# A hybrid encoder layer on one core: the last blocks of three products in seven instead of eight block products, and their streamed hi parts made by ScalarE

## The chip, the cores and the metric

The kernel runs on one core of one Trainium2 chip. The metric is the device time of one execution in microseconds (us); smaller is better. Five engines work side by side, each through a queue of its own in the order in which the program was built: TensorE (PE, with its weight loads as PEld), VectorE (DVE), ScalarE (ACT), GpSimd (POOL) and SyncE (SP, which issues nearly all DMAs). They wait for one another through semaphores only.

## What is computed

One layer on 2048 tokens of width 1024, all in fp32, cut to what matters:

```python
u = rms_norm(h, g_mix_pre);  z = u @ w_in
y = concat(swa_with_sinks(...z...), hgrn2(...z...)) @ w_out          # out projection
h = h + rms_norm(y, g_mix_post)
u = rms_norm(h, g_x_pre);  m = rms_norm(mem, g_mem)
y = softmax((u @ wq) (m @ wk).T per head) (m @ wv) @ wo              # cross-attention, 4 heads, 256 memory tokens
h = h + rms_norm(y, g_x_post)
u = rms_norm(h, g_ffn_pre)
y = (silu(u @ w_gate) * (u @ w_up)) @ w_down
h = h + rms_norm(y, g_ffn_post)
```

## The kernel before

**Precision.** TensorE multiplies in the fast fp32r format. Each fp32 matrix is split into a hi part (rounded to fp32r) and a lo part (the rest); a product is hi x hi + hi x lo + lo x hi, three matmuls. In `products` these are lines 1122, 1123 and 1124. A split is `split2`: the hi part at line 985 (`engine="A"`, ScalarE) or line 987 (POOL), then the lo part by a VectorE subtraction at line 988.

**The folded cross-attention.** Before the stage of interest, `fold_cross` multiplies wq with the memory's keys and wo with its values, so that scores and values are two products with 1024 x 1024 matrices (`qk_d`, `vo_d`). Out projection, scores, values, gate/up and down are then all of one form: a resident matrix of 1024 x 1024 (or less) against a stream.

**Seven products.** A block takes 256 columns of the stream and multiplies them with the resident matrix, both cut into 2 x 2 parts. In plain form ("p", `eight`) that is eight products of parts; each has four k tiles (`nk`), so 12 matmuls of 128x512. In Strassen-Winograd form ("s", `seven`) it is seven, with sums of parts on both sides:

```python
STEPS = {"s": (1, 5, 6, 3, 7, 2, 4), "p": (1, 2, 8, 3), ...}
```

The numbers name the residents: 1, 2, 3 and 8 are parts, 5, 6, 7 and 4 are sums of parts. A step of "s" is one product, a step of "p" two. `streamed` makes the block's stream tiles `S`: for "p" four splits, for "s" four sums (line 1097) and seven splits. Five `S` buffers take turns; tiles are made two steps ahead (`upto(need[g + 2])`). `seven` copies three partial results out of PSUM (`part`, line 1137), and each job's `out` adds them on VectorE.

**Jobs.** `jobs` lists the stage: out projection (`mixed_block`), scores (`score_block`), values (`value_block`), gate/up for two halves of the tokens (`hidden_blocks`), down in three parts (`down_block`). The first three have 8 blocks of 256 tokens each. Their streams come from `tokens`. The blocks' kinds come from `kinds`: out projection's first block is "p", the last block of each of the first three jobs is "p", every other block of the stage is "s". The down and gate/up jobs already name "s" for their last blocks, and give "A" to `streamed`, so that ScalarE makes all hi parts; in the first three jobs `streamed` gives four of the seven hi parts of a block to ScalarE and three to POOL.

**Residents.** `phases` keeps seven slots for residents: four "big" and three "T" tiles. `half` loads one half of the next resident (128x1024) when a slot's last use is past; `split` splits it (ScalarE hi, VectorE lo, a 128x1024 operation each) two steps later, queued behind what the step issued before. Where a job's last block is "s" (`change`), more halves and splits are allowed for in that block and the next job's first (`fresh`). The sums 5, 7, 6 and 4 are made ahead by `combined` and loaded ready.

**Beside the products** each block has row work, spread over the following steps (`after`): root mean squares (ScalarE squares at line 1476, small POOL operations at lines 1487 to 1491), scalings and residual adds on VectorE (lines 1529, 1530, 1604, 1608, 1617), for scores the maxima (1561), exps (ScalarE, 1565) and divisions (1573), and transposes (TensorE 1381, ScalarE copy 1382). The scheduler of the framework fixes each engine's order from these when the program is built.

Of the kernel before, what the change touches and what calls it, by code (L numbers as in the profile page):

```python
# [29 lines left out]
NT = T // P  # L30
# [18 lines left out]
class Layer:  # L49
# [1121 lines left out]
    def plain(self, S, T, nk, out, keep, kind):  # L1171
# [36 lines left out]
        yield  # L1208

    def phases(self, jobs, first, prologue=None):  # L1210

        steps = [(n, i, p) for n, job in enumerate(jobs) for i, b in enumerate(job[2])
                 for p in self.STEPS[b[0]]]
        takes = [c for job in jobs for b in job[2] for c in self.TAKES[b[0]]]
# [200 lines left out]
    def jobs(self):  # L1418
        I = self.I

        def weights(src, r0, nk):
            return lambda t, i, j, k0, n: self.load(
                t, src[r0 + (i * nk + k0) * P:r0 + (i * nk + k0 + n) * P, j * 512:(j + 1) * 512]
                .rearrange("(k p) d -> p k d", p=P))

        def ffn_u(b):
            return lambda t, i, j, k0, n: self.load(
                t, self.u_d[4 * i + k0:4 * i + k0 + n, :, b * TB + j * 512:b * TB + (j + 1) * 512]
                .rearrange("k p t -> p k t"))

        def kinds(blocks, n=0, last="p"):
            return [("p" if i < n else last if i == len(blocks) - 1 else "s",) + b for i, b in enumerate(blocks)]

        def sums(name, src, nk, other=None):
            return self.sums(name, src, nk, self.extra_tile, other or self.gain_tile)

        def in_turn(*what):
            return lambda: itertools.chain.from_iterable(w() for w in what)

        qk, vo = weights(self.qk_d, 0, 4), weights(self.vo_d, 0, 4)  # L1440
        down = [(weights(I["w_down"], f0 * P, nk), f0, nk) for f0, nk in ((0, 3), (6, 4), (14, 4))]
        qk_s, vo_s = sums("qk_s", qk, 4, self.row_tile), sums("vo_s", vo, 4)
        u_s = sums("u_s", ffn_u(1), 4)
        self.u0_s = self.tc.dram_tile([4, P, 4 * 512], F32, name="u0_s")
        d_s = [sums(f"d_s{c}", src, nk) for c, (src, _, nk) in enumerate(down)]
        jobs = [(self.w_out, 4, kinds([self.mixed_block(n) for n in range(0, NT, 2)], 1), self.out_sums, {1: [qk_s[1]]}),
                (qk, 4, kinds([self.score_block(n) for n in range(0, NT, 2)]), qk_s[0], {1: [vo_s[1]]}),
                (vo, 4, kinds([self.value_block(n) for n in range(0, NT, 2)]), vo_s[0], {})]
        for b in range(NB):
            beside = {2: [in_turn(*(d[1] for d in d_s))]} if b else {4: [u_s[1]]}  # L1450
            jobs.append((ffn_u(b), 4, kinds([blk for f in range(0, NFF, 2) for blk in self.hidden_blocks(b, f)], 0, "s"),
                         u_s[0] if b else self.u0_s, beside))
        for c, (src, f0, nk) in enumerate(down):
            jobs.append((src, nk, kinds([self.down_block(c, f0, nk, n) for n in range(0, NT, 2)], 0, "s"), d_s[c][0], {}))

        return jobs
# [10 lines left out]
    def tokens(self, src, n):  # L1467

        return lambda kind: self.streamed(lambda t, j: self.load(
            t, src[n:n + 2, :, 512 * j:512 * j + 512].rearrange("i p c -> p i c")), 4, kind, tiles=True)  # L1470

    def mean_square(self, a, to):

# [291 lines left out]
```

## Time and profile before

| | |
|---|---|
| time, median of 3 runs | 2574.08 us (2572.68 to 2574.33) |
| profiled execution: time, span | 2572.97 us, 2571.3 us |
| TensorE clock granted | 0.999 |
| PE, DVE, ACT, POOL busy | 2535.4, 1764.8, 1263.9, 425.4 us |
| first matmul of out projection, scores, values, gate/up | 778.8, 952.2, 1122.9, 1295.2 us |
| first matmul of the second gate/up job | 1720.7 us |

The profile comes from one execution. A group's line names the source line, engine, operation, tile written and read, and the count; behind the bar stand busy us, mean ns of one, and the idle time of that engine just before, with what ended it. Lengths of operations that follow each other overlap a little, and a matmul's modelled length overlaps the next ones, so paces are read from start to start. Idle time of an engine that is not the bottleneck costs nothing.

### The profile page before, as it was taken

Reading aid. Unit: us, or ns where it says so; the run is one execution under the profiler, and the core shown is the slowest. Engines: PE = TensorE matmul, PEld = TensorE weight load, DVE = VectorE, ACT = ScalarE, POOL = GpSimd, SP = SyncE. Lnnn points to the kernel's source line nnn. Section 1 sums busy time; section 2 is a strip of 40 time slices with the busy share of each in tenths; the row PEclk is TensorE's granted clock in tenths of the full one; section 3 lists DMA queues with packets and bytes.
Section 4 is the critical chain, followed back from the end, with each engine's and each line's share of the span. In section 5 each row is a group of like instructions: output and inputs, shape, how many; then the busy total and the mean of one; then the engine's idle time right before and its main releaser. Section 6 shows DMA issues by size and latency. Waiting matters only on the chain.

```text
span 2571.3 us, 34876 instructions
## 1 busy us (share of the span) xinstructions
PE 2535.4 (99%) x12326; PEld 2124.0 (83%) x12326; DVE 1764.8 (69%) x2791; ACT 1263.9 (49%) x2643; POOL 425.4 (17%) x612
## 2 busy tenths in 40 slices
PE   9999999999999999999999999999999999999998
PEld 8888888878987888888778888888888888888886
DVE  7785588887556778788885655576666557574766
ACT  5563466555555565565563333344333335443543
POOL 4231334321312322212310000000000000000022
PEclk9999999999999999999999999999999999999999
DMA  5445755765887896665973622253555425464776
GB/s 189 148 164 170 205 162 163 228 198 160 262 282 276 294 310 209 221 218 198 341 244 117 205 91 74 82 205 117 186 197 196 156 94 182 165 195 106 226 178 152
DMA packets 357295, 486.36 MB, mean 189 GB/s; under 512 B 20352, under 2 KB 248704, under 8 KB 357120
## 3 DMA queue, kind: packets, MB, share of 16 engines
q1 hardware_dynamic: 351072, 462.11, 54.6%
q0 software_dynamic: 6048, 22.02, 4.9%
q8 instruction: 97, 1.59, 0.3%
q14 instruction: 78, 0.64, 0.1%
HBM read 317.34 MB, written 166.72 MB: 188 GB/s over the span
## 4 chain that ended last, share of the span: by engine, by line
PE 82%; DMA 6%; DVE 6%; ACT 2%; issue 2%; POOL 1%; SPq 1%; DVEq 0%; POOLq 0%; ACTq 0%
PE psm L1122 22%; PE psm L1124 22%; PE psm L1123 22%; PE psg L157 2%; PE psg L156 2%; PE psg L158 2%; PE pss L1381 1%; DMA x<-in_w_out_dram 1%; DVE S L988 1%; DMA y_d<-sg 1%; DMA u_d<-row 1%; DVE T L988 0%; SPq L75 0%; DMA qk_s<-extra 0%; DVE S L808 0%
## 5 line engine op out<-in xcount | busy, mean ns | idle before, releaser
L1123 PE MATMUL psm<-T,S 128*128 128x512 f32 x2680 | 1042.9, 390 | 1.4 <-DVE T L988 1.4
L1122 PE MATMUL psm<-T,S 128*128 128x512 f32 x2680 | 1035.2, 391 | 4.9 <-ACT part L1137 3.4
L1124 PE MATMUL psm<-T,S 128*128 128x512 f32 x2680 | 1030.5, 390 | 4.9 <-DVE S L988 4.9
L1122 PEld LDWEIGHTS psm<-T,S 128*128 128x128 f32 x2680 | 503.0, 188 | 113.3 <-ACT part L1137 6.0
L1124 PEld LDWEIGHTS psm<-T,S 128*128 128x128 f32 x2680 | 503.1, 188 | 111.4 <-DVE S L988 7.0
L1123 PEld LDWEIGHTS psm<-T,S 128*128 128x128 f32 x2680 | 503.2, 188 | 106.4 <-DVE T L988 3.8
L985 ACT ACTIVATE S<-sum 128x512 fp32r<-128x512 f32 (+1 forms) x330 | 198.6, 619 | 364.1 <-PE psm L1124 260.9
L988 DVE TENSOR_TENSOR S<-sraw,S 128x512 fp32r<-128x512 f32 (+1 forms) x315 | 214.6, 689 | 229.8 <-ACT S L985 216.4
L988 DVE TENSOR_TENSOR S<-sum,S 128x512 fp32r<-128x512 f32 (+1 forms) x388 | 259.1, 677 | 47.1 <-ACT S L985 32.6
L1137 ACT ACTIVATE part<-psm 128x512 f32<-128x512 f32 x285 | 168.9, 596 | 244.9 <-PE psm L1124 223.6
L985 ACT ACTIVATE S<-sraw 128x512 fp32r<-128x512 f32 (+1 forms) x268 | 165.2, 617 | 110.0 <-PE psm L1124 99.4
L1509 POOL DMA_DIRECT2D y_d<-row x16 | 14.0, 877 | 1077.4 <-DVE row L1695 1026.6
L988 DVE TENSOR_TENSOR T<-row,T 128x1024 fp32r<-128x1024 f32 (+1 forms) x112 | 131.8, 1189 | 35.9 <-ACT T L985 34.1
L157 PE MATMUL psg<-u,whi 128*128 128x512 f32 x320 | 127.8, 399 | 0.0
L158 PE MATMUL psg<-u,wlo 128*128 128x512 f32 x320 | 127.1, 397 | 0.0
L156 PE MATMUL psg<-u,whi 128*128 128x512 f32 x320 | 127.1, 397 | 0.0
L1476 ACT ACTIVATE junk<-row 128x512 f32<-128x512 f32 x160 | 99.7, 625 | 45.7 <-DVE row L1498 27.2
L985 ACT ACTIVATE T<-row 128x1024 fp32r<-128x1024 f32 (+1 forms) x112 | 113.6, 1032 | 8.6 <-DMA row<-d_s 4.3
L987 POOL TENSOR_SCALAR S<-sum 128x512 fp32r<-128x512 f32 x58 | 49.4, 851 | 300.1 <-PE psm L1124 240.9
L1646 DVE TENSOR_TENSOR row<-psm,part 128x512 f32<-128x512 f32 x66 | 43.7, 688 | 68.3 <-PE psm L1124 68.2
L1655 DVE TENSOR_TENSOR part<-psm,part 128x512 f32<-128x512 f32 x66 | 43.8, 688 | 60.2 <-PE psm L1124 60.0
L1695 DVE TENSOR_TENSOR row<-psm,part 128x512 f32<-128x512 f32 x72 | 49.1, 688 | 49.5 <-PE psm L1124 49.4
(364 smaller groups left out, 3715.6 us busy)
## 6 DMA issues: line engine op xcount, KB each, us to landing
sraw<-in_w_gate_dram SPq DMA_DIRECT2D x44, 512.0 KB, 3.6
sraw<-in_w_up_dram SPq DMA_DIRECT2D x44, 512.0 KB, 3.7
hid_d<-row SPq DMA_DIRECT2D x44, 512.0 KB, 2.7
sraw<-hid_d SPq DMA_DIRECT2D x32, 512.0 KB, 4.1
sraw<-in_w_in_dram SPq DMA_DIRECT2D x44, 256.0 KB, 3.6
z_d<-pair SPq DMA_DIRECT2D x20, 512.0 KB, 3.0
raw<-in_w_in_dram SPq DMA_DIRECT2D x20, 512.0 KB, 4.6
z_d<-z SPq DMA_DIRECT2D x20, 512.0 KB, 4.0
```

The source lines that it names most:

```text
L156: nc.tensor.matmul(ps, ah, bh, start=(i == 0), stop=False)
L157: nc.tensor.matmul(ps, ah, bl, start=False, stop=False)
L158: nc.tensor.matmul(ps, al, bh, start=False, stop=(i == n - 1))
L985: self.nc.scalar.activation(hi, raw, AF.Copy)
L987: self.nc.gpsimd.tensor_scalar(hi, raw, 1.0, 1.0, ALU.mult, ALU.mult)
L988: self.nc.vector.tensor_tensor(lo, raw, f32(hi), ALU.subtract)
L1122: nc.tensor.matmul(ps, s[:, 0, k, :], t[:, 0, k, :], start=st, stop=False, **kw)
L1123: nc.tensor.matmul(ps, s[:, 0, k, :], t[:, 1, k, :], start=False, stop=False, **kw)
L1124: nc.tensor.matmul(ps, s[:, 1, k, :], t[:, 0, k, :], start=False, stop=sp, **kw)
L1137: nc.scalar.activation(t, ps, AF.Copy)
L1476: self.nc.scalar.activation(junk, a, AF.Square, scale=float(D) ** -0.5, accum_out=to)
L1695: nc.vector.tensor_tensor(d, a, b, ALU.add)
```

## The change

In `jobs` the last blocks of out projection, scores and values become "s"; in `tokens` the stream of these three jobs is given to `streamed` with "A".

```diff
-        jobs = [(self.w_out, 4, kinds([self.mixed_block(n) for n in range(0, NT, 2)], 1), self.out_sums, {1: [qk_s[1]]}),
-                (qk, 4, kinds([self.score_block(n) for n in range(0, NT, 2)]), qk_s[0], {1: [vo_s[1]]}),
-                (vo, 4, kinds([self.value_block(n) for n in range(0, NT, 2)]), vo_s[0], {})]
+        jobs = [(self.w_out, 4, kinds([self.mixed_block(n) for n in range(0, NT, 2)], 1, "s"), self.out_sums, {1: [qk_s[1]]}),
+                (qk, 4, kinds([self.score_block(n) for n in range(0, NT, 2)], 0, "s"), qk_s[0], {1: [vo_s[1]]}),
+                (vo, 4, kinds([self.value_block(n) for n in range(0, NT, 2)], 0, "s"), vo_s[0], {})]
...
         return lambda kind: self.streamed(lambda t, j: self.load(
-            t, src[n:n + 2, :, 512 * j:512 * j + 512].rearrange("i p c -> p i c")), 4, kind, tiles=True)
+            t, src[n:n + 2, :, 512 * j:512 * j + 512].rearrange("i p c -> p i c")), 4, kind, "A", tiles=True)
```

What follows from it in the code: with "s" last, `steps` grows by three a job, resident 8 is fetched a second time in none of the three jobs, and `change` and `fresh` hold at these three changes of job too. The parts of the program that the scheduler orders around them move as well.

## The prediction

> **What bounds the kernel now.** I read the page's engine line first.
>
> ```profile
> PE 2535.4 (99%) x12326; PEld 2124.0 (83%) x12326; DVE 1764.8 (69%) x2791; ACT 1263.9 (49%) x2643; POOL 425.4 (17%) x612
> ```
>
> TensorE works 99% of the span, so the time is the number of its matmuls plus a few waits. Two rows of TensorE's timeline, twelve matmuls (one block product of four k tiles, three matmuls each) apart, give the pace:
>
> ```profile
> 797.84 0.39 PE L1122 MATMUL psm<-T,S 128*128 128x512 f32 x1
> ...
> 800.56 0.39 PE L1122 MATMUL psm<-T,S 128*128 128x512 f32 x1
> ```
>
> That is 2.72 us a product, 0.227 us a matmul; the 0.39 is the pipelined length of one. Next the busy times by stage, cut at the first matmul of each job (columns: length; busy PE, weight loads, DVE, ACT, POOL; clock; DMA share, GB/s), and what PE waited for in the first three jobs:
>
> ```profile
> 778.80:952.20 173.40, 170.62 (x801) 141.00 (x800) 125.04 (x147) 97.36 (x215) 45.88 (x68) 1.00 0.84 291
> 952.20:1122.90 170.70, 170.70 (x823) 142.41 (x822) 137.24 (x234) 100.74 (x236) 47.12 (x66) 1.00 0.71 238
> 1122.90:1295.20 172.30, 169.33 (x798) 139.69 (x797) 145.79 (x183) 104.66 (x232) 48.12 (x66) 1.00 0.74 245
> 1295.20:1720.70 425.50, 423.98 (x1882) 349.75 (x1881) 259.83 (x379) 174.16 (x303) 4.37 (x6) 1.00 0.43 142
> ...
> PE psm L1124 <- DVE S L988: 4.9, 4, 2.3
> PE psm L1123 <- DVE T L988: 1.4, 3, 0.8
> PE psm L1122 <- ACT part L1137: 0.7, 1, 0.7
> ```
>
> The rows are out projection, scores, values, first gate/up job. In the first three VectorE is 72 to 85% busy and PE waits 7.0 us in all; in the fourth VectorE is 61% busy. So TensorE sets the time, but VectorE stands close behind it exactly in the three jobs that the change touches. What it does there, by form, from 830 to 1300 us (count, then busy us and mean ns):
>
> ```profile
> L1476 ACT ACTIVATE junk<-row 128x512 f32<-128x512 f32 x112 | 69.6, 623 | 26.7 <-DVE row L1498 24.8 <-DVE row L1608 0.9 <-DVE row L1557 0.2
> L988 DVE TENSOR_TENSOR S<-sum,S 128x512 fp32r<-128x512 f32 x75 | 51.0, 684 | 9.0 <-POOL S L987 7.6 <-ACT S L985 0.7
> L988 DVE TENSOR_TENSOR S<-sraw,S 128x512 fp32r<-128x512 f32 x68 | 48.9, 722 | 20.1 <-ACT S L985 12.4 <-POOL S L987 7.6
> L988 DVE TENSOR_TENSOR T<-row,T 128x1024 fp32r<-128x1024 f32 x40 | 48.4, 1219 | 11.4 <-ACT T L985 11.3
> L1382 ACT ACTIVATE row<-pss 128x512 f32<-128x512 f32 x84 | 46.2, 591 | 7.8 <-PE pss L1381 7.8
> L985 ACT ACTIVATE T<-row 128x1024 fp32r<-128x1024 f32 x43 | 44.5, 1057 | 0.0
> L1137 ACT ACTIVATE part<-psm 128x512 f32<-128x512 f32 x56 | 32.3, 593 | 29.0 <-PE psm L1124 28.6 <-DVE row L1557 0.3
> L987 POOL TENSOR_SCALAR S<-sum 128x512 fp32r<-128x512 f32 x36 | 30.8, 855 | 166.0 <-PE psm L1124 135.4 <-DVE S L988 15.7 <-DVE sum L1097 8.1
> L987 POOL TENSOR_SCALAR S<-sraw 128x512 fp32r<-128x512 f32 x27 | 26.5, 983 | 46.6 <-PE psm L1124 37.7 <-issue 6.8 <-ACT part L1137 2.1
> L985 ACT ACTIVATE S<-sum 128x512 fp32r<-128x512 f32 x40 | 24.9, 630 | 37.0 <-PE psm L1124 31.4 <-issue 5.5
> L1565 ACT ACTIVATE row<-row,x_mr,r_x 128x256 f32<-128x256 f32 x42 | 24.9, 594 | 32.9 <-POOL x_mr L1563 32.7
> L1573 DVE TENSOR_SCALAR row<-row,mc 128x256 f32<-128x256 f32 x64 | 19.3, 364 | 0.2
> L1530 DVE TENSOR_TENSOR row<-row,row 128x1024 f32<-128x1024 f32 x14 | 18.7, 1362 | 0.0
> L1529 DVE SCALAR_TENSOR_TENSOR row<-row,q_r,g 128x1024 f32<-128x1024 f32 x14 | 18.1, 1332 | 6.1 <-POOL q_r L1491 6.1
> L1617 DVE SCALAR_TENSOR_TENSOR row<-row,q_r,extra 128x1024 f32<-128x1024 f32 x14 | 17.8, 1303 | 3.7 <-DMA out_dram<-row 1.8 <-DMA row<-h_d 1.4 <-POOL q_r L1491 0.6
> L1604 DVE SCALAR_TENSOR_TENSOR row<-row,q_r,g 128x1024 f32<-128x1024 f32 x14 | 17.7, 1305 | 2.7 <-POOL q_r L1491 2.7
> L1608 DVE TENSOR_TENSOR row<-row,row 128x1024 f32<-128x1024 f32 x14 | 17.3, 1274 | 0.0
> L1561 DVE TENSOR_REDUCE x_mx<-row 128x2 f32<-128x512 f32 x21 | 14.2, 678 | 0.1
> ```
>
> **Term 1, TensorE.** A last block as "p" has 8 products, as "s" 7. Three blocks lose one each: 3 x 12 = 36 matmuls x 0.227 = 8.2 us, all on the path.
>
> **Term 2, the change of job.** With "p" last, the residents 5, 6, 7 and 4 of the old job are dead a whole block before its end, and the next job's 14 resident halves are split over the last two steps of the seventh block, the long last block and six steps of the next job, 8/7 x 21.0 + 23.7 = 47.7 us by the block times worked out below. With "s" last a slot comes free only step by step within the last block; by the rules in `phases` the 14 splits then stand in eleven steps, from two steps into the last block to step 5 of the next job, as they already do between the two gate/up jobs. Against that, the second fetch of resident 8 goes (six splits, eight loads in the three jobs), and the last blocks get three more stream tiles, four more sums and three more output adds each, ten VectorE operations of 128x512.
>
> How much VectorE needs in eleven steps: in its timeline at the change between the gate/up jobs
>
> ```profile
> 1714.52 1.22 DVE L988 TENSOR_TENSOR T<-row,T 128x1024 fp32r<-128x1024 f32 x1
> 1715.66 0.68 DVE L1657 TENSOR_TENSOR row<-part,row 128x512 f32<-128x512 f32 x1
> ...
> 1718.00 0.68 DVE L1655 TENSOR_TENSOR part<-psm,part 128x512 f32<-128x512 f32 x1
> 1718.60 0.68 DVE L988 TENSOR_TENSOR S<-sum,S 128x512 fp32r<-128x512 f32 x1
> ```
>
> operations follow each other 0.60 (128x512) and 1.14 us (128x1024) apart: 0.08 less than their lengths, which I take off everywhere. An "s" block has 7 lo parts, 4 sums and 3 output adds, 14 x 0.60 = 8.4. Out projection adds 2 x (1.25 + 1.28), 13.5 in all; scores 4 x 0.60 + 8 x 0.28, 13.1; values 2 x (1.225 + 1.19 + 1.22), 15.7; gate/up about two operations more, 9.6. The 14 splits are 16.0. An "s" block of the first three jobs lasts about 21.0 on PE: the scores row's 170.7 less 684 x 0.227 leaves 1.9 a block for transposes beside 84 x 0.227 = 19.1; a "p" block 96 x 0.227 + 1.9 = 23.7.
>
> Five steps of the old job and six of the new, against PE's time: out projection to scores 9.6 + 11.2 + 16.0 = 36.8 against 33.0, 3.8 too much; scores to values 9.4 + 13.5 + 16.0 = 38.9, 5.9 too much; values to gate/up 11.2 + 8.2 + 16.0 = 35.4 against 31.4, 4.0 too much; together 13.7. Between the gate/up jobs the same sum is 31.1 against 30.0, and there the whole FFN part's waits hold one line for that change:
>
> ```profile
> PE psm L1122 <- ACT part L1137: 0.7, 1, 0.7
> ```
>
> So an excess of 1.1 is absorbed without a wait for VectorE. I take 13.7 - 3 x 1.1 = 10.4 us of new waits. Bounds: below, each change of job like the one shown, 0.7 and a refilled pipeline (0.39 - 0.23 = 0.16), 2.6 in all; above, nothing absorbed and ScalarE's excess on top (rival B). The loads of the halves crowd too, on SP's queue among the blocks' loads and stores; they are issued two steps (5.4 us) ahead of their splits, and "ACT T" above has no idle time before it, so I count nothing; with that cover gone, splits would wait for DMAs, which the 0.74 to 0.84 of DMA share allows. What goes: the 1.4 and the 0.7 above, which lie at these changes, with four refills 2.75.
>
> **Term 3, hi parts.** 24 blocks x 3 = 72 hi parts go from POOL (0.855, 0.983) to ScalarE (0.63): 45 us more on an engine that is 56 to 61% busy in the three jobs, so about 68%. Each waits there for a stream buffer that PE frees (the L985 rows: PE psm L1124); behind it in ScalarE's queue stand squares, exps and transpose copies, for which POOL's small root chain and VectorE's row work wait. That is hidden outside the changes of job; there it is rival B. What it gives: a hi part is ready 0.3 us earlier, and VectorE is no longer held up beside POOL:
>
> ```profile
> 1249.26 1.16 POOL L987 TENSOR_SCALAR S<-sum 128x512 fp32r<-128x512 f32 x1 [8.46 <-PE psm L1124]
> ...
> 1249.85 1.10 DVE L1413 TENSOR_TENSOR row<-row 128x512 f32<-128x512 f32 x1
> ```
>
> The VectorE operation took 1.10 instead of the 0.68 of the rows further up. In the groups this is thin: L988 from sraw 722 against 684, 68 x 0.04 = 2.6; L1530 1362 against 1219 for T, 14 x 0.14 = 2.0 us in 470. The four waits "PE psm L1124 <- DVE S" (4.9, with refills 5.5) lie inside blocks, behind such tiles: 4 x 0.3 for the hi parts and 2 x 0.4 for held operations, 2.0 comes back (between 0 and 5.5).
>
> The Trainium skill, "SBUF — State Buffer", section "Who interferes with whom", says that a VectorE instruction with two SBUF inputs contends with a GpSimd instruction that reads SBUF, and that the later one blocks fully. The pair of rows agrees in kind; by the rule taken whole, as an estimate, 72 x 0.855 = 62 us of VectorE or POOL time would come free and term 3 would be the whole 5.5, while the groups show a few us.
>
> **Sum.** -8.2 + 10.4 - 2.75 - 2.0 = -2.5 us. On the profiled execution (2572.97, span 2571.3) that is 2570.4; on the median of 2574.08, which lies 1.1 above it, 2571.6, -0.1%.
>
> **Rivals.** 0.2% (5.1 us) is about what a measurement of this kernel can tell from no change. *A, the change of job stays as cheap as between gate/up jobs*: T tiles are needed in turn, and row work can slip behind them into the next block. For: the low bound; VectorE's 20% idle before the changes. Against: VectorE's 85% in the values job, and waits for T there although "p" gave it 47.7 us. Time: -8.2 + 2.6 - 2.75 - 2.0 = -10.4, 2563.7. *B, ScalarE becomes the pace at the changes of job, slower*: every lo part needs its hi part first. ScalarE's block is 3 x 0.593 + 0.6 + 8 x 0.623 + 4 x 0.591 + 7 x 0.63 = 14.1 in out projection and values, about 13.3 in scores (8 exps), 7.4 in gate/up, and 14 x 1.057 = 14.8 of splits: 36.3, 36.4 and 31.2 against 33.0, 33.0 and 31.4, 6.7 too much. It decides where VectorE, itself late, must wait for hi parts that are late too, so that both excesses add; the hi parts then bring nothing: -8.2 + 10.4 + 6.7 - 2.75 = +6.2, 2580.3. Against: POOL's part of the root chain gets quicker. *That the change doesn't do what it says* is out: the built program has 36 matmuls and 72 POOL operations fewer.
>
> **Chances.** A holds the faster side, 0.37: the forecast needs only half of the new waits to vanish. B holds the slower side, 0.23. The forecast lies between, 0.40 within 0.2%, its own range 2569 to 2579. All cases: low is A with a little more of term 3 (2562.5), high is B and a little more (2581.5).
>
> **What would show it.** Right: PE's L1122 to L1124 with 12 instructions fewer each; "last" blocks of some 21 us instead of 23.7; new PE waits for DVE T and S in the 30 us around the first matmul of scores, values and gate/up, about 10 us; fewer waits inside blocks. Wrong: those waits under 4 us (A), or ScalarE without idle time there and VectorE waiting for "ACT T" and "ACT S" (B); or new waits spread over all 24 blocks, which would make term 3 a cost.

## The result, and the profile after

The changed kernel takes 2583.86 us (median of 6 runs, 2577.91 to 2586.86) where the kernel before takes 2573.53 beside it (2570.75 to 2574.8): a ratio of 1.0035 on record, interval 1.0021 to 1.0049 (the quotient of the two medians is 1.0040). It is slower, where 2571.6 was forecast, and lies above the range of the prediction (2562.5 to 2581.5). The profiled execution has a span of 2581.2 us against 2571.3. The engine line of the page after:

```profile
PE 2535.8 (98%) x12290; PEld 2123.3 (82%) x12290; DVE 1763.9 (68%) x2815; ACT 1300.8 (50%) x2721; POOL 365.8 (14%) x540
```

The 36 matmuls are gone (12290 against 12326), the 72 POOL operations too, and ScalarE has 36.9 us more. TensorE's busy time did not fall. What TensorE waits for from 780 to 1350 us is the same view of which the prediction shows the three lines of before (us in total, times, longest):

```profile
PE psm L1122 <- ACT part L1137: 6.2, 2, 5.7
PE pss L1381 <- DVE row L1617: 4.9, 1, 4.9
PE psm L1124 <- DVE S L988: 3.2, 3, 1.5
PE psm L1122 <- ACT T L985: 2.2, 3, 0.9
PE psm L1122 <- ACT S L985: 1.2, 1, 1.2
PE psm L1123 <- DVE T L988: 1.0, 1, 1.0
PE pss L1381 <- ACT row L1382: 0.6, 1, 0.6
PE psm L1122 <- DVE row L1498: 0.3, 1, 0.3
```

7.0 us became 19.6, and more than half of it are two single waits of 5.7 and 4.9 us. Where they lie is read from three stretches, each from the first matmul of a job's last block to the first matmul of a block well inside the next job: out projection to scores (to scores' third block), scores to values (to values' fourth), values to gate/up (to gate/up's fourth). The windows of before, then of after; the columns are those of the prediction's stage rows:

```profile
928.68:994.19 65.51, 65.51 (x313) 54.34 (x312) 54.30 (x69) 47.50 (x97) 17.21 (x29) 1.00 0.74 260
1099.37:1185.38 86.01, 85.27 (x398) 70.16 (x397) 72.47 (x102) 53.31 (x113) 16.39 (x25) 1.00 0.61 214
1271.61:1358.94 87.33, 85.81 (x398) 69.89 (x397) 67.40 (x83) 59.27 (x112) 10.45 (x15) 1.00 0.72 246
```

```profile
924.17:996.93 72.76, 65.46 (x302) 53.13 (x300) 56.70 (x75) 52.96 (x111) 13.55 (x24) 0.95 0.70 242
1102.11:1192.89 90.78, 86.04 (x386) 68.88 (x385) 71.08 (x106) 59.03 (x121) 11.25 (x15) 0.98 0.59 194
1279.77:1368.69 88.92, 84.00 (x385) 69.18 (x384) 70.04 (x88) 58.23 (x111) 10.08 (x15) 0.98 0.71 240
```

Each stretch has 12 matmuls (2.7 us) fewer and should have fallen to 62.8, 83.3 and 84.6; it rose by 7.3, 4.8 and 1.6. Length less PE's busy time, summed over the three rows, went from 2.3 to 17.0 us. The rest of the 9.9 us between the spans is small: 1.4 less before out projection, 3.2 less in its first seven blocks, 0.7 more in values, 0.1 more behind.

**Out projection to scores.** TensorE's timeline:

```profile
953.73 0.40 PE L1124 MATMUL psm<-T,S 128*128 128x512 f32 x1
959.87 0.79 PE L1122 MATMUL psm<-T,S 128*128 128x512 f32 x1 [5.74 <-ACT part L1137]
960.46 0.63 PE L1123 MATMUL psm<-T,S 128*128 128x512 f32 x1
960.88 0.63 PE L1124 MATMUL psm<-T,S 128*128 128x512 f32 x1
...
963.02 0.43 PE L1123 MATMUL psm<-T,S 128*128 128x512 f32 x1
```

It waits until ScalarE has copied a partial result out of a PSUM bank. ScalarE's timeline says why the copy is late:

```profile
947.44 1.06 ACT L985 ACTIVATE T<-row 128x1024 fp32r<-128x1024 f32 x1 [1.79 <-DMA row<-qk_s]
...
956.70 1.07 ACT L985 ACTIVATE T<-row 128x1024 fp32r<-128x1024 f32 x1
957.65 0.64 ACT L1476 ACTIVATE junk<-row 128x512 f32<-128x512 f32 x1
958.17 0.21 ACT L1476 ACTIVATION_READ_ACCUMULATOR junk<-row 128x1 f32 x1
958.26 1.06 ACT L985 ACTIVATE T<-row 128x1024 fp32r<-128x1024 f32 x1
959.21 0.60 ACT L1137 ACTIVATE part<-psm 128x512 f32<-128x512 f32 x1
```

From 947.4 on there is no idle time ahead of any row: hi parts of the new residents (T), hi parts of the stream, squares and transpose copies stand in one queue, the copy behind them. The chain of work that ended last (`--critical`) runs on ScalarE all the way from 950.2 us to this copy. VectorE is not full there, which the first of these windows (947 to 960) shows: ScalarE 12.56 of 13 us, VectorE 8.23.

```profile
947.00:960.00 13.00, 5.80 (x28) 4.13 (x26) 8.23 (x9) 12.56 (x25) 3.65 (x7) 0.86 0.95 336
960.00:963.60 3.60, 3.60 (x10) 2.84 (x11) 3.00 (x4) 2.20 (x3) 1.16 (x1) 0.57 0.87 286
963.60:968.00 4.40, 4.40 (x25) 3.73 (x24) 4.40 (x5) 2.70 (x4) 0.00 (x0) 1.00 0.80 280
```

The other two rows show a second cost. After the wait the granted clock is 0.57 for 3.6 us, and the matmuls follow each other 0.43 apart instead of 0.23 (the rows at 960.46 and 960.88). With the refilled pipeline 1.8 us are lost on top of the wait.

**Values to gate/up.** A chain over four engines, from the timeline of all of them:

```profile
1306.61 0.61 ACT L1476 ACTIVATE junk<-row 128x512 f32<-128x512 f32 x1
...
1307.39 0.61 POOL L1487 TENSOR_TENSOR q_v<-q_s 128x2 f32<-128x2 f32 x1 [18.30 <-ACT junk L1476]
...
1308.40 1.22 POOL L1491 TENSOR_TENSOR q_r<-q_w,mhalf 128x2 f32<-128x2 f32 x1
...
1309.65 2.48 DVE L1617 SCALAR_TENSOR_TENSOR row<-row,q_r,extra 128x1024 f32<-128x1024 f32 x2 [0.60 <-POOL q_r L1491]
...
1311.08 1.79 PE L1381 MATMUL pss<-ident,row 128*128 128x128 f32 x8 [4.86 <-DVE row L1617]
```

A late square on ScalarE holds POOL's root, the root VectorE's scaling, and the scaling eight transposes that stand at the head of TensorE's queue, with the products behind them.

**Scores to values.** Many short waits, 4.7 us in all, half of them between 1129 and 1136 us. VectorE has no idle row from 1123.75 to 1140.2. TensorE waits for a hi part of a resident, and four lo parts of residents stand in one go in VectorE's queue behind it:

```profile
1133.32 1.04 ACT L985 ACTIVATE T<-row 128x1024 fp32r<-128x1024 f32 x1
1134.41 0.98 PE L1122 MATMUL psm<-T,S 128*128 128x512 f32 x2 [0.91 <-ACT T L985]
...
1134.95 4.63 DVE L988 TENSOR_TENSOR T<-row,T 128x1024 fp32r<-128x1024 f32 x4
```

### The profile page after: what moved, and what is told of

Same layout as the page of the kernel before. It is cut to its first block, busy times and chain, and to the rows that moved or that the text cites. A ratio compares the mean times of both kernels' runs of the same rounds, so it can differ in the third digit from the quotient of the medians.

```text
span 2581.2 us, 34806 instructions
## 1 busy us (share of the span) xinstructions
PE 2535.8 (98%) x12290; PEld 2123.3 (82%) x12290; DVE 1763.9 (68%) x2815; ACT 1300.8 (50%) x2721; POOL 365.8 (14%) x540
## 4 chain that ended last, share of the span: by engine, by line
PE 83%; DMA 5%; DVE 4%; ACT 3%; issue 3%; POOL 1%; SPq 1%; DVEq 0%; POOLq 0%; ACTq 0%
PE psm L1122 23%; PE psm L1124 23%; PE psm L1123 23%; PE psg L158 2%; PE psg L157 2%; PE psg L156 2%; PE pss L1381 1%; DMA row<-d_s 1%; ACT junk L1476 1%; DVE S L988 1%; DMA x<-in_w_out_dram 1%; DMA z<-in_w_out_dram 1%; DVE T L988 1%; SPq L75 1%; ACT T L985 1%
## 5 line engine op out<-in xcount | busy, mean ns | idle before, releaser
L1122 PE MATMUL psm<-T,S 128*128 128x512 f32 x2668 | 1034.2, 392 | 14.3 <-ACT part L1137 9.1
L1124 PE MATMUL psm<-T,S 128*128 128x512 f32 x2668 | 1026.9, 390 | 3.2 <-DVE S L988 3.2
L1122 PEld LDWEIGHTS psm<-T,S 128*128 128x128 f32 x2668 | 501.7, 188 | 124.2 <-ACT part L1137 13.0
L1124 PEld LDWEIGHTS psm<-T,S 128*128 128x128 f32 x2668 | 501.6, 188 | 110.1 <-DVE S L988 6.0
L985 ACT ACTIVATE S<-sum 128x512 fp32r<-128x512 f32 (+1 forms) x382 | 231.0, 619 | 385.7 <-PE psm L1124 287.0
L988 DVE TENSOR_TENSOR S<-sum,S 128x512 fp32r<-128x512 f32 (+1 forms) x400 | 268.1, 679 | 53.0 <-ACT S L985 47.9
L1137 ACT ACTIVATE part<-psm 128x512 f32<-128x512 f32 x294 | 174.2, 597 | 251.0 <-PE psm L1124 229.8
L985 ACT ACTIVATE S<-sraw 128x512 fp32r<-128x512 f32 (+1 forms) x297 | 183.0, 618 | 98.8 <-PE psm L1124 94.1
L988 DVE TENSOR_TENSOR T<-row,T 128x1024 fp32r<-128x1024 f32 (+1 forms) x106 | 124.1, 1185 | 32.8 <-ACT T L985 32.3
L985 ACT ACTIVATE T<-row 128x1024 fp32r<-128x1024 f32 (+1 forms) x106 | 107.6, 1028 | 8.8 <-DMA row<-d_s 4.4
L812 ACT ACTIVATE S<-S,w_mn 128x256 f32<-128x256 f32 (+1 forms) x128 | 63.1, 497 | 30.9 <-DVE w_mn L808 30.5
```

The source lines that it names most:

```text
L812: nc.scalar.activation(s[:, r, o:], s[:, r, o:], AF.Exp, bias=mn[:, i:i + 1], scale=-1.0, accum_out=den[:, i:i + 1])
L985: self.nc.scalar.activation(hi, raw, AF.Copy)
L988: self.nc.vector.tensor_tensor(lo, raw, f32(hi), ALU.subtract)
L1122: nc.tensor.matmul(ps, s[:, 0, k, :], t[:, 0, k, :], start=st, stop=False, **kw)
L1124: nc.tensor.matmul(ps, s[:, 1, k, :], t[:, 0, k, :], start=False, stop=sp, **kw)
L1137: nc.scalar.activation(t, ps, AF.Copy)
```

## The experiments

The stretches named below are the three of the last section, in their order. A stretch in which nothing was changed repeats well from program to program (65.5 to 65.7 us for the first in the four with eight products in out projection's last block), while the first matmul of out projection comes between 776.1 and 786.7 us in the profiled executions, though no edit is aimed at what runs ahead of it. So parts are compared by stretches, and times by their medians and intervals. What was expected names theories: S, ScalarE's queue is too full at the changes of job; V, VectorE's work is too much there; H, the hi parts on ScalarE are the cost; O, the order of the row work, whose late results stand ahead of products in TensorE's queue.

**The two halves of the change.** Only the first or only the second hunk of the diff was kept.

```diff
 s_only:  kinds(..., 1, "s") / (..., 0, "s") / (..., 0, "s") as changed;  streamed(..., kind, tiles=True)
 a_only:  kinds(...) as before;  streamed(..., kind, "A", tiles=True)
```

> Last blocks in seven products, hi parts of the streamed blocks shared with POOL as before. If ScalarE's queue is the pace at the three changes of job (theory S), five hi parts fewer stand in it in each stretch, some 3 us each, so TensorE's waits there shrink from about 20 us in all to about 10: 2574 to 2578 us, quicker than with the whole change. If VectorE's excess is the pace (theory V), nothing is taken off it and POOL holds it up again: 2583 to 2587. If the hi parts on ScalarE cost in all 24 blocks (theory H), the 8.2 us of matmuls come out whole: under 2570.

> All hi parts of the streamed blocks by ScalarE, last blocks in eight products as before. Theories S and V: the changes of job have 47 us again, so waits there as before the change, and the waits inside out projection's blocks (2.5 us at 830 us) go as they went with the whole change: 2570 to 2573. Theory H: the loss is here, 2580 or more.

Seven products alone: 2590.06 against 2576.37, ratio 1.0056 (1.0040 to 1.0072); stretches 70.9, 90.1, 89.7. Hi parts alone: 2572.83, ratio 0.9989 (0.9978 to 1.0000); stretches 65.7, 86.0, 87.4 and 2.2 us less in out projection's first seven blocks. So the hi parts are at most a small gain and H falls; the loss is in the last blocks. With POOL's hi parts back the time was above what any theory had. S had expected TensorE's waits to fall to about 10 us; they were 18.6 where the changed kernel has 19.6, which speaks against ScalarE's stream hi parts being what tips it. The groups of the kernel with hi parts alone show the mechanism that the prediction gave for them, from 830 to 1300 us as there:

```profile
L988 DVE TENSOR_TENSOR S<-sraw,S 128x512 fp32r<-128x512 f32 x68 | 46.3, 685 | 7.8 <-ACT S L985 7.7
L1530 DVE TENSOR_TENSOR row<-row,row 128x1024 f32<-128x1024 f32 x14 | 16.6, 1219 | 0.0
```

722 ns became 685, 1362 became 1219: with POOL's hi parts gone VectorE is no longer held beside them.

**One last block at a time**, each with the hi parts on ScalarE:

```diff
 s_out_a: "s" in mixed_block's kinds alone
 s_val_a: "s" in value_block's kinds alone
 s_sco_a: "s" in score_block's kinds alone
```

> As a_only, but out projection's last block in seven products. Theory S: the change from out projection to scores, where ScalarE's sum was 3.3 us too much, takes the 10 us of waits that the changed kernel shows there, less 2.7 of matmuls: 6 to 8 us slower than a_only. Theory V, by its sum of 3.8 less 1.1: within 1 us of a_only.

> As a_only, but the values' last block in seven products. By the sums ScalarE has no excess at this change (31.2 against 31.4) and VectorE 4.0: theory S gives a gain of 1 to 2.7 us against a_only, theory V a loss of 0 to 2. If the queue's order matters more than its sum (squares, then POOL's root, then VectorE's scaling, then transposes on TensorE), the 5 us wait for the values' rows comes back and it is 2 to 4 us slower than a_only.

> "A" for all three jobs, "s" last in scores alone. If the parts add up, scores' part of the change is what is left of the changed kernel's loss: changed kernel +10 us over the kernel before, of it -3 for the hi parts, +9.5 out projection, +6.5 values, so about -3 for scores: the time is 2 to 4 us below that of the version with only the hi parts. If the three last blocks cost each other nothing but are each slow by themselves, scores' stretch (first matmul of its last block to that of the third block of values) is 90 us instead of 86.0 and the time is 4 us above that version.

Ratios 1.0023 (1.0011 to 1.0034), 1.0015 (1.0002 to 1.0028) and 1.0008 (0.9999 to 1.0017). In the stretches out projection's brings 73.1 where the hi parts alone have 65.7, the 7.4 us that S had and V had not. Values' brings 88.6 where they have 87.4, and the 4.9 us wait at the transposes: a loss where ScalarE's sum had a gain, by the order of its queue. Scores' brings 87.2 where they have 86.0, much less than the 90.8 of the changed kernel. The expectation that scores' part would be a gain missed. The three do not add up to the whole: these traces also have 1207 to 1209 us behind the last stretch, the kernel before and the changed one 1204. With out projection's alone it is one wait of 3.9 us between the down jobs, and again for a copy that stands in ScalarE's queue, here (2421.45 us) behind a hi part whose load came 2.24 us late. No line of the edit names that place; the built order moves there with the rest of the program.

**Without the squares.** ScalarE's squares of the last two blocks of out projection and of values are left out, a constant stands for their sums.

```diff
+        if leave:                       # n >= 12
+            nc.gpsimd.memset(to, 0.5)
+        else:
+            self.mean_square(d, to)
```

> The changed kernel, but in the last two blocks of out projection and of values ScalarE makes no squares: a constant written by POOL stands for the sums of squares (32 ScalarE operations of 0.62 us fewer, 20 us). Theory S (ScalarE's queue at the change of job is too full): the stretch from the first matmul of out projection's last block to that of scores' third block falls from 72.8 to 66 us or less, that of values to gate/up from 88.9 to 86 or less, the one of scores to values stays at 90.8; the time falls by 8 to 11 us. Theory V (VectorE's work is too much there): all three stretches stay within 1 us. Theory O (one chain: late squares hold the root, the root holds VectorE's row work, and the transposes wait at the head of TensorE's queue): values to gate/up falls, out projection to scores falls by 2 us or less.

2573.9 us, ratio 0.9983 (0.9973 to 0.9993). Its three stretches:

```profile
930.30:992.99 62.69, 62.69 (x302) 52.17 (x301) 55.02 (x73) 41.37 (x71) 12.28 (x18) 1.00 0.74 271
1098.16:1188.97 90.81, 86.04 (x385) 68.75 (x384) 71.44 (x107) 58.91 (x120) 11.09 (x15) 0.98 0.59 194
1275.73:1360.83 85.10, 82.19 (x385) 68.01 (x384) 70.01 (x88) 48.37 (x76) 8.88 (x11) 1.00 0.75 253
```

72.8 fell to 62.7 and 88.9 to 85.1, within half a microsecond of what the products alone need, with VectorE's work all but the same (55.0 of 62.7 us busy). The stretch without squares, scores to values, did not move. S holds at the first change of job, where O had 2 us or less; at values to gate/up O had a fall too, and the run does not tell the two apart. V is out at both.

**POOL for half of the residents' hi parts**, those of scores, values and the first gate/up job.

```diff
-            self.split2(t, dst[:, 0, a:b], dst[:, 1, a:b], "A")
+            self.split2(t, dst[:, 0, a:b], dst[:, 1, a:b], "P" if pool and a else "A")
```

> The changed kernel, but the hi part of the second half of each resident of scores, values and first gate/up is made by POOL instead of ScalarE (21 operations of 1.06 us off ScalarE, about 7 us at each change of job; POOL, 16% busy, takes longer for each). Theory S: each of the three stretches falls by 2 to 6 us, the wait for a part copy goes, the time is 6 to 12 us shorter. Theory V: VectorE is held up beside POOL and its lo parts come no earlier: the stretches stay the same or grow by up to 3 us each. Theory O: the wait at the transposes in the values to gate/up stretch goes, since the squares come sooner; out projection to scores stays.

2586.07, ratio 1.0037 (1.0024 to 1.0050); stretches 72.5, 85.0, 92.0. No theory had this. TensorE's waits from 780 to 1350 us:

```profile
PE psm L1123 <- DVE T L988: 8.8, 6, 2.4
PE psm L1122 <- ACT part L1137: 3.9, 3, 2.9
PE psm L1122 <- ACT T L985: 1.9, 3, 1.4
PE psm L1124 <- DVE S L988: 1.8, 2, 1.6
```

The wait for the copy is smaller and the wait at the transposes is gone, as S and O said; but the lo parts of residents are now late (8.8 instead of 1.0 us). Scores to values fell by 5.8 us, close to the 83.3 of its products; values to gate/up rose by 3.1. In all, taking 7 us a change of job off ScalarE brought nothing with POOL, a slower engine, ahead of VectorE in its place.

**All row work of the last blocks four steps later.**

```diff
+            for _ in range(4 if n == NT - 2 else 0):   # in after(), all three blocks
+                yield
```

> The changed kernel, but the row work of the last block of out projection, scores and values (roots, scalings, residual adds, second squares, divisions, transposes) starts four steps (about 11 us) later; nothing is left out. Theories S and V: the same operations stand in the same 30 us, only less of it ahead of the residents; residents come up to 5 us earlier, of each change of job about half of the loss goes: stretches 69 to 70, 88, 87, time 6 to 8 us shorter. Theory O: out projection to scores 66 to 68, values to gate/up 84 to 86, since no transpose stands ahead of a product while its row is late: 8 to 13 us shorter. If the change of job is limited by when slots come free and by the loads, nothing moves.

2585.1, ratio 1.0031 (1.0019 to 1.0043); stretches 73.7, 89.2, 88.3, both large waits still there. A miss. What the code says of it: the second squares and transposes that stand in those microseconds are those of the block before the last, and the first squares of the last block are made in its `out`, which this edit does not move.

**The residents' hi parts in the order of need.** The built queue of ScalarE at scores to values, in the changed kernel (ahead of each line its place in the queue; T: residents by number, in the order in which TensorE needs them):

```
1127 L985 Activation T_1841_11760<-row_1849_11801 128x1024
...
1129 L985 Activation T_1854_11830<-row_1856_11833 128x1024
...
1131 L985 Activation T_1854_11830<-row_1855_11831 128x1024
...
1135 L985 Activation T_1841_11760<-row_1842_11761 128x1024
```

The first half of T_1841 stands behind both halves of T_1854: that is the 1133.32 row above, for which TensorE waited, and VectorE's queue has the lo parts of both its halves and of T_1854's first half behind it. With scores alone in "s" T_1841's first half does not stand behind T_1854.

```diff
+            ...                             # last: the hi part that was issued before this one
+            with (self.tc.issue_after(last) if any(i is last for i in traced) else contextlib.nullcontext()):
+                self.split2(t, dst[:, 0, a:b], dst[:, 1, a:b], "A")
+            ...
```

> The changed kernel, but ScalarE makes the hi parts of the residents' halves in the order in which TensorE needs them. In the changed program the scheduler issues some out of turn: at out projection to scores three halves stand behind a half of a later resident, at scores to values one half each behind one and behind two halves of a later resident; with scores alone in "s" the second of these is absent, and that stretch is 87.2 instead of 90.8. Theory Q (the order in ScalarE's queue makes the scores to values loss): that stretch falls from 90.8 to 87.5 or less; out projection to scores falls by 0 to 2 us from 72.8, values to gate/up (no half out of turn) stays at 88.9 within 0.5; time 3 to 6 us shorter. Rival W (the amount of ScalarE and VectorE work alone counts): all three within 0.7 us.

2580.09 against 2574.8, ratio 1.0017 (1.0008 to 1.0026). Two of its stretches:

```profile
926.62:997.22 70.60, 65.67 (x302) 53.64 (x301) 56.11 (x73) 52.65 (x112) 12.11 (x24) 0.95 0.70 251
1102.49:1190.16 87.67, 84.18 (x385) 67.42 (x384) 71.08 (x107) 58.41 (x120) 11.54 (x15) 1.00 0.59 200
```

72.8 to 70.6 and 90.8 to 87.7, values to gate/up 89.3: about as Q, the order in ScalarE's queue, had it (two of its three bounds missed by 0.2), and W, the amount of work alone, is out. Behind the last stretch stand 1202.4 us here, and 1202.5 in all later versions with the halves in order.

**The first squares of the last blocks later**, with the halves in order: they and the row work behind them are made seven steps on, in the next job; then also the second squares of the block before.

```diff
-            self.squared(y[i][...], a, b, ss[0][...])
+            self.squared(y[i][...], a, b, None if n == NT - 2 else ss[0][...])
...
+            for q in range(7 if n == NT - 2 else 0):
+                if q == 7 - 2 or q == 7 - 1:
+                    self.mean_squares(y[q - 7 + 2], q - 7 + 2, ss[0])
+                yield
 late_sq7_7 adds, ahead of the second squares:
+            for _ in range(7 if n == NT - 4 else 0):
+                yield
```

> The halves in order of need, and in the last block of out projection and of values the four first squares and all row work behind them five to seven steps later (nothing left out). Theory S: four of the eight squares in ScalarE's full stretch go, 2.4 us of 4.2, and with them half of what leaving all squares out gave: out projection to scores 67 to 69 us, values to gate/up 86 to 87.5. Theory that the block before the last holds TensorE (its late second squares, root, and transposes): values to gate/up stays at 88.9, out projection to scores falls under 1 us.

> As the one before, and the second squares of the block before the last and what follows on them seven steps later too, so that no square stands in the twelve steps around the two changes of job. Theory S: as with all squares left out, out projection to scores 63 to 65, values to gate/up 85 to 86, and with the halves in order scores to values 87 or less: time 2562 to 2568 where the kernel before has 2575. Rival: the postponed squares and transposes only meet the residents of the next job's first steps, five steps later: the loss moves into the stretch behind, steady1 grows from 105.2 to 108 or more, and the time stays above the kernel before.

The first: 2567.29, ratio 0.9968 (0.9956 to 0.9981), stretches 61.2, 87.6, 84.4, with 108.1 instead of 105.2 us in scores' blocks behind the first stretch, where the postponed transposes now lie. It gained more than S had for half of the squares: 70.6 + 105.3 became 61.2 + 108.1, 6.6 us, when four squares of 0.61 left the full queue. They are not alone in it: the block's row work on VectorE went too (52.5 us busy in the first stretch, 56.1 with the order alone), though row work moved four steps without its squares had gained nothing above. The wait at the transposes went with them. The second: 2569.28, ratio 0.9977 (0.9967 to 0.9986), stretches 64.5, 87.7, 82.7 and 107.1, no better as a whole, where S had 2562 to 2568: in its first stretch two waits of 1.2 and 1.0 us for a resident stand at scores' second block, where the version before has none.

**What each part brings**, in four versions of the one with postponed squares: without the order of need; with eight products in scores' last block; with POOL for half of values' residents; without the divisions of scores' last two blocks.

```diff
 late_only:      split2(..., "A") without issue_after
 late_sco_p:     kinds([self.score_block(n) for n in range(0, NT, 2)])
 late_pool_val:  "P" if pool and a else "A", pool only for values' residents
 late_no_div:    for h in range(4 if n < 12 else 0):  tensor_scalar_mul(...)
```

> Postponed squares and row work of the last blocks as in the version before, but the residents' hi parts in the order that the scheduler chose (some out of turn). If order and squares act separately: scores to values back at 90 to 91 us, values to gate/up 84 to 85 as with both, out projection to scores and the four blocks after it together 169 to 172, time 3 to 5 us above the version with both (2570 to 2572). If the order is all: out projection to scores above 70. If the squares are all: time within 2 us of the version with both.

> The version with postponed squares and halves in order, but scores' last block in eight products again. By the stretches: scores to values 86.0 (as in the kernel before and the two others with eight there) instead of 87.6, all else as in that version: 1 to 2 us faster than it, 2565.5. If seven products there pay once the order is right, it is 1 us or more slower.

> The version with postponed squares and halves in order; of the residents of values POOL makes the hi part of the second halves (7 of 14). If ScalarE's queue holds scores to values: 87.6 falls to 85 to 86, time 2 us shorter. If VectorE holds it: 87.6 or more, since VectorE's lo parts are not fewer and run beside POOL.

> The version with postponed squares and halves in order, but in the last two blocks of scores VectorE makes no divisions (reciprocals and products with them left out, 2.4 us of VectorE a block). If VectorE holds scores to values: 87.6 falls by 2 to 3 us to 85 or 85.5. If ScalarE does: 87.6 within 0.6.

Without the order: 2568.55, ratio 0.9984 (0.9974 to 0.9994), stretches 61.3, 88.5, 83.7 and 1204.9 behind, where 1202.5 stand with it. In the traces the order is worth 3.7 us from out projection on, though not where it was expected (scores to values came to 88.5 and not 90); the intervals of the two times overlap, so that squares and order act separately is likely and not shown.

POOL for values' residents: 0.9976 (0.9965 to 0.9987), 88.8 where 87.6 was, with a new wait of TensorE for hi parts of residents (4.8 us in two), so this run does not say what ScalarE's share is worth there. Without divisions: 0.9964 (0.9952 to 0.9975), 86.9, a gain of 0.7 for the 2 to 3 that V had. So the cause of the 4 us that scores to values still loses over its products stays open. Two things point at ScalarE: of TensorE's waits in that stretch with the squares postponed, 3.4 us, 2.3 are for a hi part of the stream and for copies; and in the earlier run with POOL for half of the residents the stretch was 85.0, with waits of 2.3 us.

Eight products in scores' last block: 2563.28 against 2573.32, ratio 0.9961 (0.9946 to 0.9975), the fastest measured, though its interval overlaps that of the version with seven there. Its stretches and all its waits from 780 to 1350 us (four lines stand ahead in this kernel: L1126 to L1128 are L1122 to L1124 of the others, L1141 is L1137):

```profile
925.85:986.66 60.81, 60.72 (x277) 49.59 (x276) 52.26 (x70) 47.10 (x97) 17.36 (x18) 1.00 0.75 263
1094.73:1180.36 85.63, 85.59 (x397) 70.08 (x396) 70.11 (x102) 58.31 (x124) 7.06 (x15) 1.00 0.62 213
1266.41:1350.77 84.36, 82.22 (x385) 67.83 (x384) 70.67 (x89) 58.48 (x111) 10.80 (x15) 1.00 0.74 250
```

```profile
PE psm L1128 <- DVE S L988: 2.0, 2, 1.3
PE psm L1127 <- DVE T L988: 1.5, 1, 1.5
PE psm L1126 <- ACT part L1141: 0.7, 1, 0.7
```

19.6 us of waits became 4.2 and no stretch shows a lowered clock.

## Why the prediction was wrong

**Term 1 (8.2 us, TensorE) was right**: 36 matmuls fewer, and where the waits are taken away the first stretch falls to 62.7, the 65.5 of before less 2.7.

**Term 3 (2.0 us, hi parts) was about right**, in size and cause: 2.2 us in out projection's first blocks with the hi parts alone, 3.2 in the changed kernel, and the VectorE lengths above. About 1 us of that may not be theirs: with seven products alone, POOL's hi parts kept, the same blocks were 1.1 shorter. The whole price that the prediction worked out, as an estimate, from the rule of the Trainium skill, "SBUF — State Buffer", section "Who interferes with whom", 5.5 us, was too much.

**Term 2, the change of job, was mis-sized, and at two of the three changes the engine in it was the wrong one.** It had 10.4 us of new waits less 2.75 of old ones, 7.65. The three stretches lost 10.0, 7.5 and 4.3 us over their fewer products, 21.8. The step that failed is the price of the change of job by VectorE's demand over eleven steps, 3.8, 5.9 and 4.0 too much. Averaged over 30 us, neither engine's excess predicts a wait of 5.7: what counted was ScalarE's queue without a gap from 947.4 on, in which a copy that TensorE's next bank hung on stood last. Of the 21.8 us, 14.7 are idle time of TensorE (2.3 became 17.0) and some 5 are slow matmuls after waits. Four things that the sum did not have show in it, and overlap: the queue order ("ACT part"), the transposes ahead of the products, hi parts out of turn (3.1 us at scores to values, 2.2 at out projection to scores), and the half clock after the waits (1.8, 1.6 and 1.8 us by the starts of the matmuls in the three stretches). At scores to values, 4 of the 7.5 us have no cause shown. The loads counted at nothing cost one visible wait of ScalarE, the 1.79 us ahead of a hi part at 947.44.

**Rival B** had the direction and, at the first change, the engine and its sign: ScalarE without idle time, and VectorE waiting for "ACT T" and "ACT S" (12.0 us in that stretch, 7.9 before). Its price of 3.3 us at the first change was an excess over eleven steps as well, added to a VectorE excess that the run without squares excludes there; 2580.3 was 3.6 us short. **Rival A** failed on "as cheap as between gate/up jobs": there no squares and transposes stand in the queues (none from 1700 to 1745 us in the trace before). What the prediction named as the sign of term 2, new waits of about 10 us for DVE T and S, was 4.2 in all, where 6.3 were before.

## What to carry to other kernels

When two stages overlap, look at the queue of each engine in that place and ask what a copy that frees a PSUM bank, or a transpose that stands ahead of products, is queued behind; demand averaged over the overlap hides it. Work that nobody needs soon (here the squares of a stage's last block) can be moved out of the overlap, and the order in which a scheduler puts ready work can be tied to the order of need; together they turned a change of +0.35% into a kernel at -0.3%. A built program shows its queues before it runs, and the halves out of turn could have been read there.

## What was not expected of the hardware

In a wait of 5.7 us (the granted clock is 0.50 from 959 to 960), after one of 4.9 us (0.57 from 1311 to 1315), and after the short waits around 1134 (four matmuls from 1133.5 to 1136.6 us, where 13 would fit at 0.227), the clock fell to half for some 3 us of matmuls inside a kernel that is 98% busy: 0.57 in the window of 960 to 963.6, with 0.43 us between matmuls instead of 0.23. A wait of about 5 us so costs a third more than it shows. The Trainium skill, "TensorE: Matmul & The Clock Gate", section "What's actually happening", says that the clock is gated to half by default and after an idle window of about 3.4 us, and is released by sustained activity; the traces agree on the release, with 3.2 us from the first matmul at 959.87 to the first that follow at full pace, from 963.02 on. The waits of up to 1.5 us in the last version left the clock at 1.00 in all three windows. The length of a wait does not decide it alone: with POOL for half of the residents, a wait of 2.4 us was followed by a clock of 0.50 (955.8 to 959.2), while after the 2.3 us of the kernel before, at 830, it stayed at 1.00.
